# Two heads of dilated attention side by side, and one 512-column product for the values of two patterns

## The chip, the cores and the metric

The kernel runs on one core of a Trainium2 chip. The metric is the device time of one execution in microseconds (us), lower is better.

## The reference, cut to what matters

Two transformer-like layers of a first block run first, then a second block with an FFN, a mixing part and another FFN, all on 512 tokens of 1024 features in float32. The change lies in the mixing part of the second block, in its dilated attention:

```
ATTN_PATTERNS = ((128, 1), (512, 4), (2048, 16))     # window, dilation; 4 heads of 64 in each pattern
...
logits = jnp.einsum('bqghd,bgqkhd->bghqk', qb, kb) * scale + bias[None, :, :, None, :]
logits = jnp.where(valid[None, :, None], logits, -jnp.inf)
lse = jax.nn.logsumexp(logits, axis=-1)
probs = jnp.exp(logits - lse[..., None])
out = jnp.einsum('bghqk,bgqkhd->bqghd', probs, vb)
mix = jax.nn.softmax(lse, axis=1)
return jnp.einsum('bghq,bqghd->bqhd', mix, out).astype(q.dtype)
```

The queries, keys and values of the three patterns are columns of one projection `u @ w_in`: 256 columns (4 heads of 64) for each of the three, in each pattern.

## The kernel before, in words

Activations are kept transposed, features on the 128 partitions and 512 tokens along the row, as two parts `hi` and `lo` whose sum is the float32 value (tiles `hn` in the mixing part). Weights come from DRAM in pieces of 512 KB (`raw`), which ScalarE and VectorE split into `whi` and `wlo` (lines 259 and 260). A product of two split operands is three matmuls, lines 291, 292 and 293 (`three`).

`featmajor` gives a product with features on the partitions: a piece of the weights is what is loaded into the array (the stationary operand) and 512 tokens stream through. `tokmajor` gives a product with tokens on the partitions, which the values need: 128 tokens of `hn` are loaded into the array and 256 columns of the weights stream. For 8 slices of the features, 4 blocks of tokens and 3 matmuls that is 96 matmuls per pattern. The first pattern takes its blocks of 128 tokens as they stand. The second and third take every fourth token, so the loaded operand is read with a step of four elements:

```
view = None if p == 0 else (lambda a, tb: a.rearrange("p (i r) -> p r i", r=4)[:, tb, :])
```

`dilated(p)` works through a pattern's 4 heads, two to a tile `m`: the first head of the tile lies on partitions 0 to 63 and the second on 64 to 127. For each head and each block `b` of 128 queries there is one step: a float32 matmul for the logits (line 1425, contraction over 64 rows, 128 or 256 keys wide, called QK below), bias and row minimum on VectorE (line 1428), exponential on ScalarE (line 1430), a transposition on TensorE (line 489, one per 128 keys), a copy of it by ScalarE (line 1435), and the product with the values (line 1437, 64 columns of the array, called AV below). Each float32 matmul of QK and AV is two records in the trace. In all there are 48 QK (36 of 128 keys and 12 of 256) and 60 AV, in 36 groups of one and 12 groups of two.

Results in PSUM use eight banks: four in turn (`pj`) for the large products, two in turn (`lt`) for the logits and transpositions, one each for the others.

`together` sets the order in which the work is written down: the large products (`mix_products`) are its main line, and after each of them as many steps of the attention (one per 2.2 units of cost) and of the state space part (one per 5) are written as its cost pays for; a large product counts 10. A scheduler then fixes one order of instructions per engine. `shares` weighs the patterns' results at the end and hands them to the product `wup`, which is on the main line. Tiles of the tag `h` (eight in turn) hold a pattern's bias, Q, K and V.

Of the kernel before, what the change touches and what calls it, by code (L numbers as in the profile page):

```python
# [11 lines left out]
AF = mybir.ActivationFunctionType  # L12
# [5 lines left out]
P = 128  # L18
# [7 lines left out]
# ---------------------------------------------------------------- column orders  # L26
# [14 lines left out]
def first_chunks():  # L41
    """256 columns of w_in per chunk (-1 is a zero column), and each chunk's place."""
# [28 lines left out]
def chunked(w, n=256):  # L71
    """[K, M] -> [M / n, 128, K / 128 * n]: a chunk of n columns, contiguous per partition."""
    k, m = w.shape
    return np.ascontiguousarray(w.reshape(k // P, P, m // n, n).transpose(2, 1, 0, 3)).reshape(m // n, P, k // P * n)


def feat(v):
    """[K] or [..., K] -> [128, ..., K / 128]"""
    v = np.asarray(v)
    return np.ascontiguousarray(np.moveaxis(v.reshape(v.shape[:-1] + (v.shape[-1] // P, P)), -1, 0))  # L80


# columns of the constants and of the vectors
# [45 lines left out]
def onehots():  # L129
    """[33, 896]: which bucket lies at each place of the three patterns' bands (row 32: NEG where none does)"""  # L130
# [55 lines left out]
def prepare(x):  # L186
# [23 lines left out]
    out["win2"] = chunked(x["w_in"][0])  # L210
    out["fnrow"] = x["final_norm"].reshape(1, D)
# [11 lines left out]
# ---------------------------------------------------------------- the program  # L223
class Prog:
# [19 lines left out]
    # -- small helpers  # L244
# [4 lines left out]
    def weights(self, src, kt, n=256, held=False):  # L249
        """src: [128, kt * n] in DRAM -> the two exact parts, [128, kt, n] each."""  # L250
# [18 lines left out]
    # the eight banks: products, then small results in two rings, then sums that stay for long  # L269
# [18 lines left out]
    def three(self, ps, a, b, first, last, **kw):  # L288
        """ps += (a[0] + a[1])^T (b[0] + b[1]) without the lowest product."""
# [5 lines left out]
    def featmajor(self, src, hT, nk=8):  # L295
        """two tiles [128 columns, 512 tokens] of a chunk of 256 columns"""
# [9 lines left out]
    def tokmajor(self, src, hT, nk=8, view=None, grans=None):  # L306
        """two tiles [128 tokens, 2 blocks, 256 columns] of a chunk of 256 columns"""
# [10 lines left out]
    def rsqrt(self, v, n, pool):  # L318
        """v: [128, n] -> 1 / sqrt(v), by Newton's steps from the bits' halving"""
# [13 lines left out]
    def squares(self, acc, first, src, eng=None, **kw):  # L333
        """acc += src^2"""
# [8 lines left out]
    def sums(self, ps, acc, nb=NB):  # L343
        """acc's sums over the partitions, a column per block of 128 tokens"""
# [4 lines left out]
    def rms(self, acc, nb=NB):  # L349
        """1 / rms per token, as columns"""  # L350
# [5 lines left out]
    def spread(self, r, nb=NB, R=None):  # L356
        """a column per block -> the row on every partition"""
# [12 lines left out]
    def scaled(self, hi, lo, x, w):  # L370
        """the parts of x * w, w a column"""
# [3 lines left out]
    def h8(self, pool=None, tag="h"):  # L375
        """the parts of a transposed activation: [hi, lo][d]"""
# [11 lines left out]
    def setup(self):  # L388
# [19 lines left out]
        # the weights of the first block's last norm and of the one that follows it  # L408
# [3 lines left out]
    def normed(self, h, chunk, R, w):  # L412
        """h <- the parts of chunk * w * R"""
# [6 lines left out]
    # ------------------------------------------------------------ first block  # L420
    def layer(self, l, xs, x, z, acc, grans=None):
        """xs: x^T in DRAM, [128, 8, 512], x the same on chip, z the parts of x times the norm's weight, acc the sums
        of x's squares; the new x^T goes to xd"""
# [48 lines left out]
    def rope(self, x, nh, b0, nb=2):  # L472
        """x: [128, nb blocks from b0, nh, 64] in place, first 16 of each 64"""
# [17 lines left out]
    def scaled_copy(self, ps, j):  # L491
        """two blocks of a product of z, each token by its 1 / rms"""
# [6 lines left out]
    def stacked_q(self, src, scale, ps=None):  # L499
        """a chunk of 4 heads of 64 -> [128 = (hi, lo), 4, 512] of q^T, after rope"""  # L500
# [30 lines left out]
    def dsa_index(self, l, ps, pi):  # L531
# [7 lines left out]
        for j in range(2):  # L539
# [12 lines left out]
            for b in range(2):  # L552
# [4 lines left out]
                # the latent, normed  # L557
# [19 lines left out]
        # scores  # L577
# [20 lines left out]
    def dsa_choose(self):  # L598
        """the scores become 0 at the 128 chosen keys and NEG at the others"""
# [15 lines left out]
    def transposed(self, tb, src, PT):  # L615
        """src: [128 t, (tb + 1) * 128 s] -> the parts PT[s, sb, t]"""
# [9 lines left out]
    def stacked_av(self, V, PT):  # L626
        """V(sb): [128 s, 128 = (v_hi | v_lo)]; -> [128, 512]"""
# [7 lines left out]
    def values(self, V, ps, j):  # L635
        """ps: [128 t, 2 blocks, 4 heads * 64] -> V[:, 2 j + b, h, (hi | lo)]"""
# [5 lines left out]
    def heads_out(self, g, i, o, Y):  # L642
        """rows 0-63 + rows 64-127 of o -> Y[(i % 2) * 64..]"""
# [6 lines left out]
    def dsa(self, l, W, g):  # L650
# [17 lines left out]
        for h in range(4):  # L668
# [9 lines left out]
            for tb in range(NB):  # L678
# [7 lines left out]
                # the negated logits, and the least of them  # L686
# [68 lines left out]
    def ml_gates(self, l):  # L755
        """log decay sums, running maxima: for all four heads"""
# [7 lines left out]
        # log_sigmoid(f) = min(f, 0) - log1p(exp(-|f|))  # L764
# [20 lines left out]
        # sums from each block's start  # L785
# [9 lines left out]
        # g[s] in the frame of each later block  # L795
# [6 lines left out]
        # running maximum, as rows  # L802
# [20 lines left out]
    def mlstm(self, l, W, u):  # L823
# [32 lines left out]
        for e in range(2):  # L856
# [37 lines left out]
            # the variance of the quotients, and its root times the quotients' factor  # L894
# [9 lines left out]
    def ml_finish(self, l):  # L904
        """the last head's quotients, normed, to DRAM"""
# [14 lines left out]
    def branch(self, l, W, g, place):  # L920
        """the branch's gated output through its weights, times the merge gate, into mixed"""
# [49 lines left out]
    def layer_out(self, l, xs, mh):  # L971
# [19 lines left out]
        # two norms in a row  # L991
# [15 lines left out]
    # ------------------------------------------------------------ second block  # L1007
# [40 lines left out]
    def last(self, g):  # L1048
        """the last products, tokens on the partitions, and the last norm"""
# [12 lines left out]
        for c in range(4):  # L1062
            # the last chunk's weights stay, so that the last block of tokens can come after the others
# [25 lines left out]
    def last_rows(self, x, fn, ss, ps, c, tbs):  # L1089
        """the products ps of the blocks tbs, chunk c, to the residual; after the last chunk the norm and the result"""  # L1090
# [32 lines left out]
    def gated(self, c, th2, br, place, mh=None):  # L1123
        """adds 2 * sigmoid(pg) * br to the chunk's two tiles of mixed"""
# [258 lines left out]
    def dilated_qkv(self, W, p):  # L1383
# [21 lines left out]
        for j in range(2):  # L1405
            nc.scalar.copy(V[:, 2 * j:2 * j + 2, :], ps[j].rearrange("p (b c) -> p b c", b=2))
# [443 lines left out]
```

## Time and profile before

| | |
|---|---|
| three timed runs | 2649.14, 2650.55 (median), 2650.63 us |
| profiled execution, first to last instruction (its span) | 2647.3 us |
| median of the timed runs less that span | 3.25 us |
| TensorE busy | 2602.0 us, 98% of the span |
| VectorE busy | 1673.3 us, 63% |
| ScalarE busy | 1181.7 us, 45% |
| GpSimd busy | 267.4 us, 10% |
| chain of work that ended last | TensorE 76%, VectorE 8%, ScalarE 3% |
| DMA | 115 GB/s over the span |

The profile's busy time of TensorE is modelled: matmuls are pipelined, and a record lasts until its result is out, so that the records of neighbours overlap. How many matmuls the engine gets through is read from the distance between the starts of neighbours, not from the mean length of a record.

### The profile page before, as it was taken

The numbers are of one execution on the slowest core, as the hardware profiler recorded it, in microseconds if no ns is written. First come the engines' busy times: TensorE is split into PE (matmuls) and PEld (weight loads), VectorE is DVE, ScalarE is ACT, GpSimd is POOL, SyncE is SP. The second block draws the span as 40 slices with busy tenths as digits, with TensorE's granted clock in tenths as the row PEclk, the third lists the DMA queues.
The fourth block names the chain that finished last, engine by engine and source line by source line (L and its number), as shares of the span: only waits on it lengthen the run. The fifth ranks groups of instructions, "written<-read, shape, count | busy, mean of one in ns | idle before, by whom it ended". The sixth has DMA issues, their size and how long they took to land.

```text
span 2647.3 us, 36272 instructions
## 1 busy us (share of the span) xinstructions
PE 2602.0 (98%) x13302; PEld 2137.8 (81%) x13302; DVE 1673.3 (63%) x3696; ACT 1181.7 (45%) x2310; POOL 267.4 (10%) x573
## 2 busy tenths in 40 slices
PE   8999999999999999999999999999999999999998
PEld 8888778788888778878888888877876787888898
DVE  8999976644699997664588664373323444555523
ACT  6565656733566665763433332243333233333322
POOL 1010000110000000010004870000000100000000
PEclk9999999999999999999999999999999999999999
DMA  6232232353322223235333334353323454322332
GB/s 191 82 108 84 85 111 98 110 176 130 110 71 87 84 89 115 97 113 173 112 128 116 131 132 134 120 179 113 106 65 115 139 170 135 119 97 96 121 92 83
DMA packets 115106, 305.58 MB, mean 115 GB/s; under 512 B 29210, under 2 KB 36506, under 8 KB 114928
## 3 DMA queue, kind: packets, MB, share of 16 engines
q1 hardware_dynamic: 87760, 236.23, 27.6%
q0 software_dynamic: 18576, 60.17, 6.5%
q10 hardware_dynamic: 8592, 6.87, 0.8%
q8 instruction: 105, 1.72, 0.3%
q14 instruction: 73, 0.60, 0.1%
HBM read 259.41 MB, written 43.79 MB: 115 GB/s over the span
## 4 chain that ended last, share of the span: by engine, by line
PE 76%; DVE 8%; ACT 3%; issue 1%; DMA 1%; SPq 0%; ACTq 0%; DVEq 0%; POOLq 0%
PE b L291 22%; PE b L292 22%; PE b L293 22%; PE b L489 2%; DVE wlo L260 1%; PE b L632 1%; DVE row L744 1%; PE b L683 1%; PE b L1425 1%; PE b L1437 1%; DVE row L743 1%; DVE row L746 1%; DVE row L742 1%; DMA row<-xd 0%; DVE keep L606 0%
## 5 line engine op out<-in xcount | busy, mean ns | idle before, releaser
L260 DVE TENSOR_TENSOR wlo<-raw,whi 128x1024 fp32r<-128x1024 f32 (+1 forms) x398 | 481.1, 1209 | 500.1 <-ACT whi L259 498.6
L259 ACT CAST whi<-raw 128x1024 fp32r<-128x1024 f32 (+1 forms) x398 | 412.9, 1037 | 634.3 <-PE b L292 482.8
L291 PE MATMUL b<-h,whi 128*128 128x512 f32 x1632 | 642.1, 393 | 0.0
L292 PE MATMUL b<-h,whi 128*128 128x512 f32 x1632 | 641.7, 393 | 0.0
L293 PE MATMUL b<-h,wlo 128*128 128x512 f32 x1632 | 640.3, 392 | 0.4 <-DVE wlo L260 0.4
L291 PEld LDWEIGHTS b<-h,whi 128*128 128x128 f32 x1632 | 307.3, 188 | 61.8 <-issue 2.3
L293 PEld LDWEIGHTS b<-h,wlo 128*128 128x128 f32 x1632 | 307.1, 188 | 61.6 <-DVE wlo L260 0.8
L292 PEld LDWEIGHTS b<-h,whi 128*128 128x128 f32 x1632 | 307.1, 188 | 60.0 <-issue 1.3
L291 PE MATMUL b<-hn,whi 128*128 128x512 f32 x320 | 129.8, 405 | 0.3 <-ACT hn L246 0.3
L293 PE MATMUL b<-hn,wlo 128*128 128x512 f32 x320 | 129.4, 405 | 0.0
L292 PE MATMUL b<-hn,whi 128*128 128x512 f32 x320 | 128.5, 402 | 0.0
L292 PE MATMUL b<-wlo,h 128*128 128x256 f32 x384 | 109.5, 285 | 0.0
L293 PE MATMUL b<-whi,h 128*128 128x256 f32 x384 | 109.2, 284 | 0.0
L291 PE MATMUL b<-whi,h 128*128 128x256 f32 x384 | 109.1, 284 | 0.0
L489 PE MATMUL b<-cst,row 128*128 128x128 f32 x452 | 88.5, 285 | 15.4 <-DVE row L746 11.1
L489 PEld LDWEIGHTS b<-cst,row 128*128 128x128 f32 x452 | 52.1, 141 | 58.7 <-issue 16.9
L1024 ACT ACTIVATE row<-row 128x512 f32<-128x512 f32 x44 | 27.8, 632 | 122.9 <-DVE row L1023 99.1
L293 PE MATMUL b<-whi,g 128*128 128x256 f32 x288 | 81.9, 284 | 0.0
L291 PE MATMUL b<-whi,g 128*128 128x256 f32 x288 | 81.6, 284 | 0.0
L292 PE MATMUL b<-wlo,g 128*128 128x256 f32 x288 | 81.6, 283 | 0.0
L291 PE MATMUL b<-yb,whi 128*128 128x512 f32 x192 | 75.9, 396 | 0.0
L293 PE MATMUL b<-yb,wlo 128*128 128x512 f32 x192 | 75.6, 394 | 0.0
(590 smaller groups left out, 5337.4 us busy)
## 6 DMA issues: line engine op xcount, KB each, us to landing
raw<-in_win_dram SPq DMA_DIRECT2D x194, 512.0 KB, 3.8
raw<-in_ffn_in_dram SPq DMA_DIRECT2D x88, 512.0 KB, 3.7
raw<-in_ffn_down_dram SPq DMA_DIRECT2D x40, 512.0 KB, 3.5
raw<-in_wbr_dram SPq DMA_DIRECT2D x24, 512.0 KB, 3.5
mxd<-fr POOLq DMA_DIRECT2D x48, 256.0 KB, 2.4
fr<-mxd POOLq DMA_DIRECT2D x48, 256.0 KB, 3.7
raw<-in_wout_dram SPq DMA_DIRECT2D x24, 512.0 KB, 3.7
yd<-row POOLq DMA_DIRECT2D x24, 256.0 KB, 2.6
```

The source lines that it names most:

```text
L259: nc.scalar.copy(hi, raw)
L260: nc.vector.tensor_sub(lo, raw, hi.bitcast(F32))
L291: mm(ps, a[0], b[0], start=first, stop=False)
L292: mm(ps, a[0], b[1], start=False, stop=False)
L293: mm(ps, a[1], b[0], start=False, stop=last)
L489: self.nc.tensor.transpose(out, in_, self.c("ident"))
L632: self.nc.tensor.matmul(o[:, c], V(sb), PT[i][:, sb, c], start=sb == 0 and i == 0, stop=sb == 3 and i == 1)
L683: nc.tensor.matmul(p[:, :nn], Q[h][:, tb * P:(tb + 1) * P], kk[i][:, :nn], start=i == 0, stop=i == 1)
L742: nc.vector.scalar_tensor_tensor(e[:, :n], e[:, :n], 1.0, st[:, :n], op0=ALU.min, op1=ALU.mult)
L743: nc.vector.scalar_tensor_tensor(sg[:, :n], sg[:, :n], 0.0, e[:, :n], op0=ALU.max, op1=ALU.add)
L744: nc.vector.tensor_tensor_scan(e[:, :n][:, ::-1], st[:, :n][:, ::-1], self.one.to_broadcast([P, n]), 1.0, op0=ALU.mult, op1=ALU.min)
L1024: nc.scalar.activation(th, t, AF.Tanh, scale=0.5)
```

## The change

The host lays the value weights of the second and third pattern out once more, as one matrix of 512 columns (`wv12`). A new function `values12` makes both patterns' values in one product at the place of the second pattern's: each loaded block of 128 tokens now meets 512 streaming columns instead of 256, over four banks of `pj` at once, and the third pattern has no value product of its own. `dilated` handles the two heads of a tile in one step, split over two turns of `together`: in the first both QK into two `lt` banks, the minimum and the exponential of each; in the second the transpositions of both into one bank, one copy for both, and the AV of both, alternating between the array's column halves 0 to 63 and 64 to 127. Comments were also taken out, which shifts line numbers by one to thirty; lines of the new kernel are 292 to 294 for the three matmuls, 1447 for QK, 490 for the transposition and 1466 for AV.

```diff
+    out["wv12"] = chunked(x["w_in"][0][:, 256 * 9:256 * 11], 512)[0]
...
-        view = None if p == 0 else (lambda a, tb: a.rearrange("p (i r) -> p r i", r=4)[:, tb, :])
-        ps = self.tokmajor(W[8 + p], self.hT, view=view)
-        V = self.m4(shape=(NB, 256))
-        for j in range(2):
-            nc.scalar.copy(V[:, 2 * j:2 * j + 2, :], ps[j].rearrange("p (b c) -> p b c", b=2))
-        self.dil[p] = (*qk, V, bias)
+        if p == 0:
+            ps = self.tokmajor(W[8], self.hT)
+            V = self.m4(shape=(NB, 256))
+            for j in range(2):
+                nc.scalar.copy(V[:, 2 * j:2 * j + 2, :], ps[j].rearrange("p (b c) -> p b c", b=2))
+            self.dv = [V]
+            yield 10.0
+        elif p == 1:
+            yield from self.values12()
+        self.dil[p] = (*qk, self.dv[p], bias)
         self.have.add(f"d{p}")
+
+    def values12(self):
+        nc = self.nc
+        V = [self.m4(shape=(NB, 256)) for _ in range(2)]
+        ps = [self.pj() for _ in range(NB)]
+        at = [h.rearrange("p (i r) -> p r i", r=4) for x in self.hT for h in x]
+        for i, gran in enumerate(self.granules(self.A["wv12"], 8, n=512, g=2)):
+            for tb in range(NB):
+                for k, hi, lo in gran:
+                    self.three(ps[tb], (at[k][:, tb, :], at[8 + k][:, tb, :]), (hi, lo), k == 0, k == 7)
+            if i % 2 == 1 and i < 3:
+                yield 10.0
+        for tb in range(NB):
+            for e in range(2):
+                nc.scalar.copy(V[e][:, tb, :], ps[tb][:, 256 * e:256 * e + 256])
+        self.dv += V
         yield 10.0
...
-            for e2 in range(2):
-                h = 2 * m + e2
-                r = slice(64 * e2, 64 * e2 + 64)
-                for b in range(NB):
-                    k0, n = (b * P, P) if p or b == 0 else ((b - 1) * P, 256)
-                    ps = self.lt()
-                    nc.tensor.matmul(ps[:, :n], Q[r, m, b * P:(b + 1) * P], K[r, m, k0:k0 + n], start=True, stop=True)
...
+            for b in range(NB):
+                k0, n = (b * P, P) if p or b == 0 else ((b - 1) * P, 256)
+                ps = [self.lt() for _ in range(2)]
+                for e in range(2):
+                    r = slice(64 * e, 64 * e + 64)
+                    nc.tensor.matmul(ps[e][:, :n], Q[r, m, b * P:(b + 1) * P], K[r, m, k0:k0 + n], start=True, stop=True)
+                L = self.row()
+                for e in range(2):
+                    h = 2 * m + e
+                    Le = L[:, e * n:(e + 1) * n]
...
-                    for j in range(n // P):
-                        nc.tensor.matmul(o[r, b * P:(b + 1) * P], V[:, k0 // P + j, h * 64:(h + 1) * 64], T[:, j * P:(j + 1) * P],
-                                         start=j == 0, stop=j == n // P - 1)
-                    yield True
...
+                yield True
+                ps = self.lt()
+                for j in range(2 * n // P):
+                    self.tr(ps[:, j * P:(j + 1) * P], L[:, j * P:(j + 1) * P])
+                T = self.row()
+                nc.scalar.copy(T[:, :2 * n], ps[:, :2 * n])
+                nj = n // P
+                for j in range(nj):
+                    for e in range(2):
+                        h = 2 * m + e
+                        nc.tensor.matmul(o[64 * e:64 * e + 64, b * P:(b + 1) * P], V[:, k0 // P + j, h * 64:(h + 1) * 64],
+                                         T[:, (e * nj + j) * P:(e * nj + j + 1) * P], start=j == 0, stop=j == nj - 1)
+                yield True
```

How this stands in the order of instructions is shown at two places. The first is TensorE's order at the start of the second pattern's value product, in the kernel before (the streaming operand is named first, the loaded one second, then the size of the result):

```order
L291 MATMUL b_3355_18387<-whi_18391,hn_17105 128x256
L292 MATMUL b_3355_18387<-wlo_18392,hn_17105 128x256
L293 MATMUL b_3355_18387<-whi_18391,hn_17109 128x256
L291 MATMUL b_3355_18387<-whi_18391,hn_17105 128x256
L292 MATMUL b_3355_18387<-wlo_18392,hn_17105 128x256
```

The same engine at the start of the shared value product, in the changed kernel:

```order
L292 MATMUL b_3313_18281<-whi_18287,hn_17105 128x512
L293 MATMUL b_3313_18281<-wlo_18288,hn_17105 128x512
L294 MATMUL b_3313_18281<-whi_18287,hn_17109 128x512
L292 MATMUL b_3313_18281<-whi_18287,hn_17105 128x512
L293 MATMUL b_3313_18281<-wlo_18288,hn_17105 128x512
```

Of such rows there were 192 in the second and third pattern's products, and there are 96 now, twice as wide.

The second place is TensorE's order in the third pattern's attention, in the kernel before (`b` is a PSUM bank, `cst` the identity of a transposition, `row` an exponential or its transposed copy, `h` the tiles of Q, K and V):

```order
L1425 MATMUL b_3585_19455<-h_18799,h_18660 128x128
L293 MATMUL b_3593_19475<-hn_17106,wlo_19480 128x512
L489 MATMUL b_3578_19414<-cst_58,row_19411 128x128
L291 MATMUL b_3594_19476<-hn_17105,whi_19479 128x512
L292 MATMUL b_3594_19476<-hn_17109,whi_19479 128x512
L1437 MATMUL b_3563_19378<-row_19416,h_19005 64x128
L1425 MATMUL b_3589_19465<-h_18799,h_18660 128x128
L293 MATMUL b_3594_19476<-hn_17105,wlo_19480 128x512
L489 MATMUL b_3587_19460<-cst_58,row_19457 128x128
L291 MATMUL b_3594_19476<-hn_17105,whi_19479 128x512
L292 MATMUL b_3594_19476<-hn_17109,whi_19479 128x512
L1437 MATMUL b_3563_19378<-row_19462,h_19005 64x128
```

And TensorE's order in the third pattern's attention in the changed kernel:

```order
L1447 MATMUL b_3492_19171<-h_18814,h_18651 128x128
L293 MATMUL b_3500_19196<-xk_19014,whi_19200 128x512
L490 MATMUL b_3490_19164<-cst_58,row_19093 128x128
L294 MATMUL b_3500_19196<-xk_19012,wlo_19201 128x512
L292 MATMUL b_3501_19197<-xk_19011,whi_19200 128x512
L293 MATMUL b_3501_19197<-xk_19013,whi_19200 128x512
L1466 MATMUL b_3471_19072<-row_19167,h_18280 64x128 x2
L1447 MATMUL b_3493_19172<-h_18814,h_18651 128x128
L490 MATMUL b_3495_19180<-cst_58,row_19175 128x128
```

Two AV that stood apart now stand together (x2). The two QK of a pair (banks 3492 and 3493) do not: the second stands behind the AV of the pair before, since it takes the bank in which that pair's transpositions were (there are two in the `lt` ring). Over all of TensorE's order the two QK of a pair are neighbours in 4 of 24 pairs, the AV stand in 18 groups of two and 6 of four, and a QK stands directly behind an AV at 18 places, where it was 23. Ahead of the attention of the first pattern and behind the start of `shares` the order of TensorE's instructions is the same in both kernels.

## Rows read from the trace of the kernel before

**Rows 1.** The page's first line: span and instructions

```profile
span 2647.3 us, 36272 instructions
```

**Rows 2.** Windows, the mixing part: length, then each engine's busy us, clock, DMA

```profile
1800.00:2060.00 260.00, 257.93 (x1185) 190.71 (x1184) 89.89 (x244) 94.24 (x245) 3.24 (x6) 0.99 0.32 98
```

**Rows 3.** Groups by line, TensorE, same stretch: one of three equal groups

```profile
L292 PE MATMUL b<-wlo,hn 128*128 128x256 f32 x64 | 26.1, 409 | 0.0
```

**Rows 4.** Timeline, TensorE, first pattern's values: first and last of 81 records

```profile
1789.91 0.28 PE L291 MATMUL b<-whi,hn 128*128 128x256 f32 x1
...
1799.52 0.28 PE L293 MATMUL b<-whi,hn 128*128 128x256 f32 x1
```

**Rows 5.** Timeline, TensorE, third pattern's values: first and last of 40 records

```profile
1931.99 0.40 PE L292 MATMUL b<-wlo,hn 128*128 128x256 f32 x1
...
1941.10 0.40 PE L292 MATMUL b<-wlo,hn 128*128 128x256 f32 x1
```

**Rows 6.** Groups by line, weight loads: 1788 to 1799 us, first pattern's values

```profile
L291 PEld LDWEIGHTS b<-whi,hn 128*128 128x128 f32 x30 | 5.6, 188 | 0.0
```

**Rows 7.** Groups by line, weight loads: 1868 to 1874 us, second pattern's values

```profile
L291 PEld LDWEIGHTS b<-whi,hn 128*128 128x128 f32 x7 | 2.3, 326 | 0.0
```

**Rows 8.** Timeline, TensorE, 512 columns: first and last of 10 records

```profile
2036.07 0.39 PE L292 MATMUL b<-hn,whi 128*128 128x512 f32 x1
...
2038.15 0.39 PE L292 MATMUL b<-hn,whi 128*128 128x512 f32 x1
```

**Rows 9.** Timeline, TensorE: a QK alone between large products

```profile
2039.69 0.40 PE L293 MATMUL b<-xk,wlo 128*128 128x512 f32 x1
2040.01 0.49 PE L1425 MATMUL b<-h,h 64*128 64x128 f32 x2
2040.43 0.50 PE L291 MATMUL b<-xk,whi 128*128 128x512 f32 x1
2040.77 0.39 PE L292 MATMUL b<-xk,whi 128*128 128x512 f32 x1
```

**Rows 10.** Timeline, TensorE: one AV (two records) alone

```profile
2041.57 0.39 PE L292 MATMUL b<-xk,whi 128*128 128x512 f32 x1
2041.89 0.43 PE L1437 MATMUL b<-row,h 128*64 128x128 f32 x2
2042.25 0.50 PE L293 MATMUL b<-xk,wlo 128*128 128x512 f32 x1
2042.59 0.39 PE L291 MATMUL b<-xk,whi 128*128 128x512 f32 x1
```

**Rows 11.** Timeline, TensorE: two AV of the same head (four records)

```profile
1830.78 0.65 PE L1437 MATMUL b<-row,h 128*64 128x128 f32 x4
```

**Rows 12.** Timeline, TensorE: a QK directly behind an AV

```profile
1917.64 0.43 PE L1437 MATMUL b<-row,h 128*64 128x128 f32 x2
1918.00 0.48 PE L1425 MATMUL b<-h,h 64*128 64x128 f32 x2
1918.42 0.51 PE L293 MATMUL b<-hn,wlo 128*128 128x512 f32 x1
```

**Rows 13.** Timeline: a QK and the exponential of its result

```profile
2015.19 0.48 PE L1425 MATMUL b<-h,h 64*128 64x128 f32 x2
...
2016.41 0.40 ACT L1430 ACTIVATE row<-row,st 128x128 f32<-128x128 f32 x1
```

**Rows 14.** Timeline: waits around 2002 us, waiting time and releaser in brackets

```profile
2002.28 1.04 ACT L259 CAST whi<-raw 128x1024 fp32r<-128x1024 f32 x1 [4.52 <-PE b L292]
...
2003.55 0.43 PE L1437 MATMUL b<-row,h 128*64 128x128 f32 x2 [1.07 <-ACT row L1435]
...
2004.85 0.48 PE L1425 MATMUL b<-h,h 64*128 64x128 f32 x2 [0.87 <-DVE st L1428]
```

**Rows 15.** Windows, behind those waits (columns as in rows 2)

```profile
2006.00:2009.00 3.00, 2.98 (x9) 1.57 (x7) 0.77 (x3) 1.72 (x6) 0.00 (x0) 0.50 0.41 156
```

More of the change, by code (lines that the diff above doesn't have):

```diff
@@ L1418, in dilated @@
             o = self.av()
-            for e2 in range(2):
-                h = 2 * m + e2
-                r = slice(64 * e2, 64 * e2 + 64)
-                for b in range(NB):
-                    k0, n = (b * P, P) if p or b == 0 else ((b - 1) * P, 256)
-                    ps = self.lt()
-                    nc.tensor.matmul(ps[:, :n], Q[r, m, b * P:(b + 1) * P], K[r, m, k0:k0 + n], start=True, stop=True)
-                    L = self.row()
+            for b in range(NB):
[8 more added lines that the diff above has]
+                    Le = L[:, e * n:(e + 1) * n]
@@ L1427, in dilated @@
                     st = st2[:, b, 0, h:h + 1]
-                    nc.vector.tensor_tensor_reduce(L[:, :n], ps[:, :n], bias[:, h, nb - n:], op0=ALU.add, op1=ALU.min,
+                    nc.vector.tensor_tensor_reduce(Le, ps[e][:, :n], bias[:, h, nb - n:], op0=ALU.add, op1=ALU.min,
                                                    accum_out=st, scale=-1.0, scalar=3.0e38)
-                    nc.scalar.activation(L[:, :n], L[:, :n], AF.Exp, bias=st, scale=-1.0, accum_out=st2[:, b, 1, h:h + 1])
@@ L1431, in dilated @@
-                    ps = self.lt()
-                    for j in range(n // P):
-                        self.tr(ps[:, j * P:(j + 1) * P], L[:, j * P:(j + 1) * P])
-                    T = self.row()
-                    nc.scalar.copy(T[:, :n], ps[:, :n])
-                    for j in range(n // P):
-                        nc.tensor.matmul(o[r, b * P:(b + 1) * P], V[:, k0 // P + j, h * 64:(h + 1) * 64], T[:, j * P:(j + 1) * P],
-                                         start=j == 0, stop=j == n // P - 1)
@@ L1439, in dilated @@
-                    yield True
+                    nc.scalar.activation(Le, Le, AF.Exp, bias=st, scale=-1.0, accum_out=st2[:, b, 1, h:h + 1])
+                yield True
[10 more added lines that the diff above has]
+                                         T[:, (e * nj + j) * P:(e * nj + j + 1) * P], start=j == 0, stop=j == nj - 1)
```

## The prediction

> **What bounds the kernel now.** I read the page first: a span of 2647.3 us [rows 1], with TensorE busy nearly all of it. The change touches one stage only, so I then read the windows of that stage, 1800 to 2060 us: TensorE is busy for 257.93 of 260 us at full clock (0.99), VectorE and ScalarE for about 90 us each [rows 2]. TensorE sets the end here. What it no longer has to do comes off the time, as long as its order holds no new waits. VectorE and ScalarE have room.
>
> Busy time alone would mislead about sizes, because records of pipelined matmuls overlap. So I went to the timeline and took distances between starts.
>
> **The value products.** The first pattern's values, whose tokens are loaded as they stand, start every (1799.52 - 1789.91) / 80 = 0.120 us [rows 4]. The third pattern's matmuls are the same size (256 streaming columns), but their loaded operand is read with a step of four elements. They start every (1941.10 - 1931.99) / 39 = 0.234 us [rows 5]. Only the load differs, and it is longer: 326 ns as against 188 ns [rows 6, 7]. So these 192 matmuls (3 x 64, [rows 3]) are held up by their loads; streaming 256 columns would let them start every 0.120 us.
>
> Matmuls with 512 columns and ordinary loads start every (2038.15 - 2036.07) / 9 = 0.231 us [rows 8]. Streaming 512 columns therefore takes as long as a stepped load, and loads run beside the streaming of the matmul before. The new product needs 96 stepped loads under 96 streams of 512 columns.
>
> - Before: 192 x 0.234 = 44.9 us.
> - After, load under stream: 96 x 0.234 = 22.5 us. Saved: 22.4 us.
> - Lower bound of the gain: the extra of a stepped load (0.234 - 0.120 = 0.114) adds to the 0.231 in full. Then 96 x 0.345 = 33.1 us, saved 11.8 us.
> - Upper bound: the stream alone counts, 96 x 0.231 = 22.2 us, saved 22.7 us.
>
> I take 22.4, because rows 5 show the load as the longer of two things that overlap, not as an addition.
>
> The Trainium skill has a rule that speaks against this gain. "TensorE: Matmul & The Clock Gate", section "LDWEIGHTS (loading the stationary operand)", gives a load's time by its columns alone, P / 1.2 ns, about 107 ns for 128, whatever the layout. By it an estimate of the saving would be 192 x 0.120 - 96 x 0.231 = 0.9 us. The trace does not agree: 326 ns against 188 ns at equal columns. The page "SBUF — State Buffer", section "Door 1: The DMA port swizzle", says that each access that crosses to a new 16-byte line pays; a step of four float32 is 16 bytes, and the trace agrees with that.
>
> The rest of this part costs nothing that shows. The same four pieces of 512 KB are read and split. One piece still serves 24 matmuls of 0.23 us, as in every other large product, so the weights need not come faster. Evictions become eight copies of 256 columns for four of 512. The next product's first bank is free once the first block of tokens is copied out, and that block ends 18 matmuls, 4.2 us, before the product does. The second V tile takes the place of the first pattern's bias, whose last reader stands well ahead in the order. Without that cover the next product would wait for two copies, under 1 us.
>
> **The attention steps.** Costs of insertions, from the start of the last large matmul before to the start of the second one after, less two ordinary distances of 0.231 us:
>
> - One AV alone: 2042.59 - 2041.57 - 0.46 = 0.56 us [rows 10].
> - Two AV of one head together: their records last 0.65 us instead of 0.43 us [rows 10, 11], so 0.56 + 0.22 = 0.78 us. A further AV in the group costs 0.22 us.
> - A QK of 128 keys alone: 2040.77 - 2039.69 - 0.46 = 0.62 us [rows 9].
> - A QK directly behind an AV: it starts 0.36 us after the AV and the large product 0.42 us after the QK [rows 12], the same distances as in rows 9 and 10. What falls away is one way out of the small shape and one way in: the large matmul after starts 0.34 us before the next instead of 0.23 [rows 9], and the one before likewise, together 0.2 us.
>
> Before, AV cost 36 x 0.56 + 12 x 0.78 = 29.5 us. After, there are 18 groups of two and 6 of four.
>
> - If the second half waits for the first as in rows 11: 18 x 0.78 + 6 x (0.78 + 2 x 0.22) = 21.4 us, saved 8.1 us.
> - If the halves run fully beside each other, a group of two costs what one costs: 18 x 0.56 + 6 x 0.78 = 14.8 us, saved 14.7 us.
>
> No row shows two halves of the array in use together. I take the middle, 11.4 us. The Trainium skill, "TensorEngine Tiling (Array Packing)", section "Key Properties", states that tiles operate independently and load and multiply in parallel. By that the 14.7 would hold; no run here shows it.
>
> The QK keep their number and mostly their cost, since only 4 of 24 pairs are neighbours: 4 x 0.2 = 0.8 us saved at least, 4 x 0.62 = 2.5 us at most. Places where a QK follows an AV fall from 23 to 18, which costs 5 x 0.2 = 1.0 us. Transpositions keep their number. ScalarE has 24 copies fewer, which is cover that nobody waits for.
>
> **New waits.** A pair's second QK now stands close ahead of the transposition that needs its exponential. In the rows of the order shown, a transposition and three or four large matmuls lie between, about 1.1 us. In the trace the way from the end of a QK (2015.67) to the end of its exponential (2016.81) is 1.14 us with the engines free [rows 13]. Ten of the 24 pairs stand so, and I price each at 0 to 0.4 us; I take 2 us in all, with 0 and 4 as bounds. TensorE's large products queue behind such a wait.
>
> The one long wait of this stage stays where it is: a cast of weights on ScalarE waits for TensorE to release a buffer, the copy of a transposition stands behind it, and TensorE waits 1.07 and 0.87 us [rows 14], after which the clock stands at half for 3 us [rows 15]. That is about 2 + 1.5 us. The changed order has two such casts ahead of an exponential at the same product, so I cost it at nothing, with 3.5 us either way as bounds.
>
> **The sum.** 22.4 + 11.4 + 0.8 - 1.0 - 2.0 = 31.6 us off the profiled execution's span of 2647.3 us. The median of the timed runs lies 3.25 us above that span, and I let that stand: 2650.55 - 31.6 = 2619 us.
>
> **The rivals.**
>
> 1. *The stepped load is not hidden under 512 columns.* Then the first part gives 11.8 and the time is about 2630 us. For it: nowhere in the trace does a stepped load meet 512 columns. Against it: rows 5 and 6, where ordinary loads vanish under 0.120 us. Chance 0.12.
> 2. *The slow spacing belongs to the product, not to the load.* Then 512 columns take 0.468 us each, the first part saves nothing, and the time is about 2641 us. The skill's rule of a load by columns alone would lead here. Against it: rows 7. Chance 0.04.
> 3. *The PSUM ring makes TensorE wait.* A pair needs both `lt` banks for its QK and one again for its transpositions, so the second QK waits for the pair before. To end slower than before by 0.2%, about what a measurement of this kernel can tell from no change (5.3 us), 37 us must be lost: 1.5 us for each of 24 pairs. A single wait of 1.07 us is the longest that the stage shows now [rows 14], and the ring has three turns per pair where it had four. At 2 us a pair the time would be 2619 + 46 = 2665 us (48 in place of the 2 allowed). Chance 0.03.
> 4. *The same waits, smaller.* At 0.6 us a pair, 14 us in place of 2, the time is 2631 us. Chance 0.08.
>
> If the halves of the array don't run side by side at all, only 3.3 us of the forecast go (2622 us); that is part of the forecast.
>
> **How the numbers follow.** The forecast, both gains with small waits, has 0.73. Its own range takes the bounds: most gain 22.7 + 14.7 + 2.5 - 1.0 + 3.5 = 42.4 (2608 us), least with hidden loads 22.4 + 8.1 + 0.8 - 1.0 - 4 - 3.5 = 22.8 (2628 us). The range given, 2608 to 2632, takes in rivals 1 and 4 as well; rivals 2 and 3 and the tails of 1 and 4 stay outside, under 2 in 10. Faster by over 0.2%: 0.95 (all but rival 3 and a small tail of 2 and 4); within: 0.02; slower: 0.03.
>
> **What would show each step.** In the changed kernel's timeline the shared value product starts every 0.23 to 0.24 us (0.345 for rival 1, 0.47 for rival 2). A group of two AV lies between 0.43 and 0.65 us long as a merged row. Waits of TensorE for ScalarE's exponential (now line 1455) before line 490 sum to about 2 us. The stage from the first QK to the last of `shares` is some 30 us shorter, and stages before and behind keep their length. The prediction is wrong if TensorE's clock falls in new places, or if waits before lines 490 or 1447 reach tens of us.

## The result, and the profile after

The changed kernel takes 2615.88 us (median of four runs, 2614.03 to 2617.0) where the kernel before took 2650.26 us beside it. The ratio is 0.9867, with a 95% interval from 0.9854 to 0.988. The forecast was 2619 us with a range of 2608 to 2632; of the 34.4 us that came off, 31.6 were forecast.

The page's first line, span and instructions (before: [rows 1]):

```profile
span 2613.5 us, 36025 instructions
```

Windows, the mixing part of the changed kernel and a short stretch inside it (columns as in [rows 2]):

```profile
1800.00:2030.00 230.00, 228.43 (x1125) 170.12 (x1124) 88.54 (x242) 93.89 (x227) 3.78 (x7) 1.00 0.37 112
2041.00:2043.50 2.50, 2.50 (x6) 1.96 (x7) 2.50 (x4) 0.47 (x1) 0.00 (x0) 0.50 0.34 105
```

TensorE is as full as before (228.43 of 230 us), VectorE and ScalarE have as much room. So the time came off as work that TensorE no longer has, and nothing else took its place as the bound. The second row is a stretch at half clock, which will matter below.

Timeline of the changed kernel, TensorE. First a QK in front of the shared value product and the product itself (line numbers are one higher than before: the value matmuls are lines 292 to 294, QK is line 1447, AV line 1466), then a group of four AV, a group of two, and two QK that are neighbours:

```profile
1856.81 0.70 PE L1447 MATMUL b<-h,h 64*128 64x256 f32 x2
1857.43 0.63 PE L292 MATMUL b<-whi,hn 128*128 128x512 f32 x1
1857.90 0.40 PE L293 MATMUL b<-wlo,hn 128*128 128x512 f32 x1
1858.13 0.40 PE L294 MATMUL b<-whi,hn 128*128 128x512 f32 x1
...
1862.42 0.39 PE L294 MATMUL b<-whi,hn 128*128 128x512 f32 x1
...
1867.51 0.66 PE L1466 MATMUL b<-row,h 128*64 128x128 f32 x8
...
1945.98 0.40 PE L293 MATMUL b<-hn,whi 128*128 128x512 f32 x1
1946.31 0.44 PE L1466 MATMUL b<-row,h 128*64 128x128 f32 x4
1946.68 0.50 PE L294 MATMUL b<-hn,wlo 128*128 128x512 f32 x1
1947.02 0.39 PE L292 MATMUL b<-hn,whi 128*128 128x512 f32 x1
...
1951.32 0.49 PE L1447 MATMUL b<-h,h 64*128 64x128 f32 x4
```

- **Value product.** From 1858.13 to 1862.42 there are 19 records one behind the other, so they start every 4.29 / 18 = 0.238 us with twice the columns. Before it was 0.234 for half of them [rows 5].
- **AV on two halves.** The group of two (x4 records) costs 1947.02 - 1945.98 - 0.46 = 0.58 us. One AV alone cost 0.56 [rows 10]. The group of four lasts 0.66 as a merged row, about what two AV of one head lasted before (0.65, [rows 11]).
- **QK on two halves.** The pair (x4) lasts 0.49, as a single one does [rows 9].

The waits of TensorE from 1800 to 2070 us (waiting instruction, releaser, us in total, times, longest):

```profile
PE b L490 <- ACT row L1455: 1.3, 1, 1.3
PE b L1501 <- DVE row L1509: 0.9, 1, 0.9
PE b L292 <- ACT xk L1254: 0.2, 1, 0.2
```

The waits of [rows 14] are gone. In their place a transposition waits once for an exponential, the matmuls of `shares` (line 1501) wait once for VectorE, and a large matmul waits briefly for ScalarE.

### The profile page after: what moved, and what is told of

Same layout as the page of the kernel before. It is cut to its first block, busy times and chain, and to the rows that moved or that the text cites. A ratio compares the mean times of both kernels' runs of the same rounds, so it can differ in the third digit from the quotient of the medians.

```text
span 2613.5 us, 36025 instructions
## 1 busy us (share of the span) xinstructions
PE 2568.2 (98%) x13206; PEld 2113.5 (81%) x13206; DVE 1673.0 (64%) x3696; ACT 1179.3 (45%) x2290; POOL 265.9 (10%) x573
## 4 chain that ended last, share of the span: by engine, by line
PE 75%; DVE 8%; ACT 3%; issue 1%; DMA 1%; SPq 0%; ACTq 0%; DVEq 0%; POOLq 0%
PE b L292 22%; PE b L293 22%; PE b L294 22%; PE b L490 3%; DVE wlo L261 1%; PE b L633 1%; DVE row L745 1%; PE b L684 1%; PE b L1447 1%; DVE row L744 1%; DVE row L747 1%; DVE row L743 1%; DMA row<-xd 0%; DVE keep L607 0%; PE b L1466 0%
```

## The experiments

### All runs in one table

Two executions of one kernel differ by some us in their profiles, and most of the reason is visible: stretches in which TensorE is granted half its clock, 3.41 us or more each. The column "half clock" sums the stretches ahead of 2600 us whose granted clock reads 0.50 in the windows. At the very end, behind 2600 us, every profile has one more such stretch, of 2.5 to 5.6 us, in which no matmul runs; that part is left in. The last column is the span less half of the column before it, an estimate of the same execution at full clock. It supposes that TensorE sets the pace in those stretches; in the changed kernel the large matmuls from 2041.41 to 2043.54 us do stand 0.43 us apart, and 0.23 elsewhere.

| kernel | median us | ratio to before on its chip | profiled span | half clock | span at full clock |
|---|---|---|---|---|---|
| before | 2650.26 | | 2647.3 | 6.8 | 2643.9 |
| before_again | 2653.70 (one run) | | 2651.8 | 13.7 | 2645.0 |
| changed kernel | 2615.88 | 0.9867 [0.9854, 0.988] | 2613.5 | 10.2 | 2608.4 |
| after_again | 2615.22 | 0.9867 [0.9854, 0.9881] | 2611.9 | 6.8 | 2608.5 |
| values_only | 2631.66 | 0.9916 [0.9902, 0.993] | 2630.4 | 10.2 | 2625.3 |
| values_again | 2632.83 | 0.9931 [0.9918, 0.9944] | 2632.5 | 13.7 | 2625.7 |
| heads_only | 2633.06 | 0.9922 [0.9909, 0.9934] | 2631.4 | 6.8 | 2628.0 |
| heads_again | 2634.75 | 0.994 [0.9927, 0.9954] | 2638.2 | 20.5 | 2628.0 |
| before_plain_loads | 2628.37 | 0.9901 [0.9886, 0.9917] | 2633.1 | 20.5 | 2622.8 |
| same_half | 2621.63 | 0.9883 [0.9869, 0.9897] | 2623.8 | 20.5 | 2613.5 |
| own_fetch | 2614.47 | 0.9859 [0.9845, 0.9872] | 2615.3 | 13.7 | 2608.5 |
| values_fetch | 2632.00 | 0.9924 [0.9912, 0.9937] | 2629.4 | 13.7 | 2622.5 |
| qk_py_bank | 2614.70 | 0.9861 [0.9846, 0.9876] | 2609.8 | 10.2 | 2604.6 |
| plain_loads_after | 2615.60 | 0.9861 [0.9847, 0.9874] | 2615.5 | 17.1 | 2606.9 |

The spans at full clock of two profiles of one kernel agree within 1.1 us for before and within 0.4 us for the other three, though their spans differ by up to 6.8 us. That makes the last column a finer measure than one span, but not an exact one. TensorE's order up to the first value matmul of the first pattern is the same in all fourteen profiles. The timeline, TensorE, at that matmul, before first and values_again second:

```profile
1786.89 0.36 PE L291 MATMUL b<-whi,hn 128*128 128x256 f32 x1
1788.61 0.36 PE L292 MATMUL b<-whi,hn 128*128 128x256 f32 x1
```

No stretch at half clock that the column counts lies ahead of it in either, and still they are 1.7 us apart. So a difference of 1 to 4 us in the last column can lie in part outside of what an edit changed.

### Each part alone: values_only and heads_only

values_only has `values12` of the changed kernel and the attention loop of the kernel before:

```diff
         for m in range(2):
             o = self.av()
-            for b in range(NB):
...
-                ps = [self.lt() for _ in range(2)]
+            for e2 in range(2):
+                h = 2 * m + e2
+                r = slice(64 * e2, 64 * e2 + 64)
+                for b in range(NB):
...
+                    ps = self.lt()
```

> Only the shared value product of the change; the attention steps are those of the kernel before. If a stepped load hides under 512 streaming columns (the profile after shows starts 0.238 us apart), 192 x 0.234 - 96 x 0.238 = 22.1 us come off: about 2628 us. If the value product owes part of its gain to the new attention steps (fewer insertions in it, fewer waits), clearly less: under 18 us, above 2632 us.

heads_only has the attention loop of the changed kernel and, for the second and third pattern, the 256-column products of the kernel before:

```diff
-        elif p == 1:
-            yield from self.values12()
...
+        view = None if p == 0 else (lambda a, tb: a.rearrange("p (i r) -> p r i", r=4)[:, tb, :])
```

> Only the attention steps of the change; each pattern has its own value product as before. If the two halves of the array run beside each other, a group of two AV costs what one cost: 14.7 us, and 2.5 us for neighbouring QK, less 1.0 us for fewer QK behind an AV and some 2 us of waits: 12 to 16 us off, 2634 to 2638 us. If the halves take turns and only the ways in and out of the small shape are saved, 6 to 9 us off: 2641 to 2644 us.

By their ratios they took 22.3 and 20.7 us off. Neither gain is absent, so rival 2 of the prediction falls. Together, though, they took more than the whole (35), while the profiled spans gave only 16.9 and 15.9 against the span of before. So one thing was open: do the parts add up? The timeline of values_only, TensorE, at the matmuls of `shares` (line 1494 there) showed a place at which its own gain was partly given back:

```profile
2057.53 2.38 PE L1494 MATMUL b<-row,cst 4*128 4x512 f32 x4 [1.16 <-DVE row L1502]
...
2060.44 0.63 PE L292 MATMUL b<-hn,whi 128*128 128x512 f32 x1
2060.86 0.63 PE L293 MATMUL b<-hn,whi 128*128 128x512 f32 x1
```

A wait of 1.16 us, and behind it large matmuls that start 0.42 us apart in place of 0.23: half clock, for 6.8 us here.

### What a stepped load costs: before_plain_loads

```diff
-        view = None if p == 0 else (lambda a, tb: a.rearrange("p (i r) -> p r i", r=4)[:, tb, :])
+        view = None
```

> The kernel before, with the second and third pattern's value products loading blocks of 128 neighbouring tokens instead of every fourth one, so that these values belong to other tokens. If the step of the load sets the spacing of 0.234 us, it falls to 0.120 us, loads to 188 ns, and 192 x 0.114 = 21.9 us come off: about 2628 us, as much as the 512-column product gives. If the spacing belongs to the product, nothing changes: 2650 us.

Timeline of this kernel, TensorE, second pattern's values: the first and last of 39 records one behind the other.

```profile
1921.35 0.28 PE L293 MATMUL b<-whi,hn 128*128 128x256 f32 x1
...
1925.86 0.28 PE L292 MATMUL b<-wlo,hn 128*128 128x256 f32 x1
```

They start every 4.51 / 38 = 0.119 us in place of 0.234 [rows 5], and at full clock the kernel is 21.7 us shorter than before (mean of that kernel's two profiles, 2644.5). The step of the load alone doubled the time of these products. The shared product gains the same amount by another way: it does not make the load shorter, it puts twice the columns over it.

### Whether the halves run together: same_half

The changed kernel, with the AV of both heads in the same column half of the array, one head behind the other; the other half of the output is zero:

```diff
+            nc.vector.memset(o[64:128, :], 0.0)
-                for j in range(nj):
-                    for e in range(2):
+                for e in range(2):
+                    for j in range(nj):
...
-                        nc.tensor.matmul(o[64 * e:64 * e + 64, b * P:(b + 1) * P], V[:, k0 // P + j, h * 64:(h + 1) * 64],
+                        nc.tensor.matmul(o[0:64, b * P:(b + 1) * P], V[:, k0 // P + j, h * 64:(h + 1) * 64],
```

> The changed kernel with the AV of both heads written to column half 0 to 63 of the array, one head after the other (the second head's rows replace the first's, the other half is set to zero). If the overlap of the halves makes the gain, a group of two takes 0.65 us as a merged record and costs 0.78 us instead of 0.57: 18 x 0.21 + 6 x 0.43 = 6.4 us more than the changed kernel, about 2622 us. If only the grouping makes it, no change: 2616 us.

Timeline, TensorE, a group of two AV:

```profile
1948.07 0.40 PE L292 MATMUL b<-hn,whi 128*128 128x512 f32 x1
1948.40 0.65 PE L1467 MATMUL b<-row,h 128*64 128x128 f32 x4
1948.98 0.50 PE L293 MATMUL b<-hn,whi 128*128 128x512 f32 x1
1949.32 0.39 PE L294 MATMUL b<-hn,wlo 128*128 128x512 f32 x1
```

The same four records cost 1949.32 - 1948.07 - 0.46 = 0.79 us on one half and 0.58 on two. At full clock the kernel is 5.1 us longer than the changed one; by the ratios it is 4.2 us longer, but the intervals overlap (0.9869 to 0.988), so the timeline is the firmer evidence. A group of two costs what one AV costs only when its AV stand on two halves: there they run beside each other.

"TensorEngine Tiling (Array Packing)", section "Key Properties", of the Trainium skill says that tiles work independently and in parallel; the trace agrees with it here (0.58 against 0.56 us for one).

### The wait in `shares`: own_fetch and values_fetch

Both take the tiles into which `shares` fetches the stored results from the `h` ring, and fetch them at its start:

```diff
+        od = []
+        for p in range(3):
+            od.append(self.m4())
+            nc.sync.dma_start(od[p], self.od[:, 2 * p:2 * p + 2, :])
...
-                o = self.fr()
-                nc.sync.dma_start(o, self.od[:, 2 * p + m, :])
+                o = od[p][:, m, :]
```

own_fetch is the changed kernel with this edit:

> The changed kernel, with the tiles into which `shares` fetches the stored results of the three patterns taken from the free places of the `h` ring, all three fetched at its start, in place of six tiles of the ring that the gates use too. Theory: in the changed kernel VectorE waited 3.13 us for such a fetch, TensorE 0.9 us for VectorE behind it, and 3.4 us at half clock stand behind that wait; with the fetches early the wait goes, and with it the half clock: 0.9 + 1.7 = 2.6 us less than the changed kernel. Rival: the half clock follows the small matmuls of `shares` (4 rows of the array) and not the wait; then 0.9 us less at most, and the clock falls near the same place. Second rival: the new bounds of the ring make other work wait, same time or slower.

Timeline of own_fetch, TensorE's rows of `shares` (lines 490 and 1505):

```profile
2024.47 1.98 PE L1505 MATMUL b<-row,cst 4*128 4x512 f32 x4
...
2027.84 1.98 PE L1505 MATMUL b<-row,cst 4*128 4x512 f32 x4
...
2030.10 0.77 PE L490 MATMUL b<-cst,sh 128*4 128x128 f32 x4 [0.29 <-DVE row L1512]
...
2032.51 3.78 PE L1505 MATMUL b<-row,cst 4*128 4x512 f32 x4
```

And its windows:

```profile
2031.00:2033.50 2.50, 2.50 (x5) 1.16 (x5) 1.89 (x3) 0.55 (x1) 0.54 (x1) 0.50 0.02 7
```

The wait went (0.29 is left of 0.89), and the time did not. In this profile the clock fell at 2030.4 us all the same, for 10.2 us, where a stretch of 3.4 us stood behind the wait in the changed kernel. The last four records of small matmuls took 3.78 us in place of 1.98. So the first rival held as far as one profile shows it: in this stage the half clock does not need the wait. What stands before it here are eight records of matmuls that use 4 rows of the array, close together. That the edit caused the longer stretch is not shown: same_half and plain_loads_after, in which `shares` keeps its wait, have a stretch of 10.2 us there too (from 2034.9 and 2024.3 us on).

values_fetch is values_only with the same edit:

> Only the shared value product, with the attention of the kernel before (as values_only), and the early fetches of own_fetch. values_only took 15.3 us off the stage in its profile where the value product alone should give 22; it showed a wait of 1.2 us in `shares` and two stretches of 3.4 us or more at half clock there. Theory: what was missing stands at that place, so with the fetches early the stage's gain rises by 1.2 + 1.7 to 1.2 + 3.4 us, 3 to 4.6 us less than values_only. Rival: what was missing lies in the value product itself or in the insertions around it; then 1 us less at most.

At full clock it is 3.0 us shorter than values_only (2622.5 against 2625.5, the mean of two). Not all of that is the edit's: at full clock the first value matmul of the first pattern, far ahead of `shares`, starts 1.4 us earlier than in those two (at 1788.86 us, less 1.7 for a stretch at half clock ahead of it, against 1788.55 and 1788.61). What is left, 1.6 us, is little more than the wait of 1.16 us. Its stretch at half clock behind `shares` lasts 10.2 us, and the timed runs show no gain (0.9924 against 0.9916 and 0.9931). The theory fell here too: that the half clock goes with the wait was wrong.

### More neighbours among the QK: qk_py_bank

```diff
-                ps = [self.lt() for _ in range(2)]
+                ps = [self.lt(), self.bank("py")]
```

> The changed kernel, with the second head's QK of a pair in the bank `py`, so that it need not wait until the pair before has left the `lt` ring. The two QK of a pair are then neighbours in 10 of 24 pairs (4 before), but a QK stands directly behind an AV at 7 places (18 before). Theory (neighbours on two halves cost as much as one, 0.62 us): 6 x 0.62 = 3.7 us saved, 11 x 0.2 = 2.2 us given back, so 1.5 us less than the changed kernel. Rival: halves save only the way in and out (0.2 us a pair), then 1 us more. Both are near what can be told apart; what the adjacent QK cost is read in the timeline.

Timeline, TensorE, a pair of QK between large matmuls:

```profile
1952.48 0.40 PE L294 MATMUL b<-hn,wlo 128*128 128x512 f32 x1
1952.81 0.49 PE L1447 MATMUL b<-h,h 64*128 64x128 f32 x4
1953.23 0.50 PE L292 MATMUL b<-hn,whi 128*128 128x512 f32 x1
1953.56 0.39 PE L293 MATMUL b<-hn,whi 128*128 128x512 f32 x1
```

Two QK on two row halves cost 1953.56 - 1952.48 - 0.46 = 0.62 us, what one cost [rows 9]. So the row halves run beside each other here, as the column halves do. The kernel is 3.8 us shorter than the changed one at full clock, of which not all need be the edit's, and its timed median (2614.70) is no different from those of own_fetch and plain_loads_after on the same chip (2614.47, 2615.60). Whether it is faster stays open. No version here beats the changed kernel by more than the measurement can tell.

### What is left of the stepped load: plain_loads_after

```diff
-        at = [h.rearrange("p (i r) -> p r i", r=4) for x in self.hT for h in x]
+        at = [h for x in self.hT for h in x]
...
-                    self.three(ps[tb], (at[k][:, tb, :], at[8 + k][:, tb, :]), (hi, lo), k == 0, k == 7)
+                    self.three(ps[tb], (at[k][:, tb * P:(tb + 1) * P], at[8 + k][:, tb * P:(tb + 1) * P]), (hi, lo), k == 0, k == 7)
```

> The changed kernel, with the value product's tokens loaded as they stand and not with a step of four elements, so that the values of the second and third pattern belong to other tokens (what is computed is changed, the number and shape of the instructions is not). Theory: the stepped load is hidden under 512 columns, so matmuls start every 0.231 to 0.235 us where they started every 0.238, 0.7 us less at most in 96, and up to 2 us where a load stands behind an insertion and has no stream over it. Rival: the load still adds in full at many places, then 5 us less or more.

Timeline, TensorE, the same place as in the changed kernel: a QK, the product behind it, and the last of 19 records that follow each other from 1858.73 us.

```profile
1857.54 0.70 PE L1447 MATMUL b<-h,h 64*128 64x256 f32 x2
1858.16 0.50 PE L292 MATMUL b<-whi,hn 128*128 128x512 f32 x1
1858.50 0.39 PE L293 MATMUL b<-wlo,hn 128*128 128x512 f32 x1
1858.73 0.39 PE L294 MATMUL b<-whi,hn 128*128 128x512 f32 x1
...
1862.92 0.39 PE L294 MATMUL b<-whi,hn 128*128 128x512 f32 x1
```

In a run of matmuls the spacing is 4.19 / 18 = 0.233 us, so the stepped load costs 0.238 - 0.233 = 0.005 us there: it is hidden. Behind an insertion it is not quite: the second value matmul starts 0.34 us after the first (1858.50 - 1858.16) with plain loads, and 0.47 (1857.90 - 1857.43) with stepped ones. The same shows at ten more places of the product: from the first matmul behind an insertion to the second it takes 0.11 or 0.12 us more than with plain loads. For the eleven places together that is 1.3 us. In all the kernel is 1.5 us shorter at full clock, and the timed runs (0.9861 against 0.9867) can't tell the two apart.

### The parts and the whole on one chip: after_again, values_again, heads_again, before_again

These are the changed kernel, the two parts and the kernel before, unchanged.

> The changed kernel once more, on one chip with its two parts alone. On the first chip the parts took 22.3 and 20.7 us off by their ratios, 43 together, and the whole took 35 off on another. By the spacings the parts give 22 (value product) and 14.7 + 2.5 - 1.0 = 16 (attention), 38 together, less 2 to 3 us of waits and half clock. Theory: the parts add up, and the first chip's runs of the kernel before lay 3 to 4 us high; then whole = sum of the parts within 3 us here. Rival: the parts take something from each other (the same idle time ended by both), then the whole stays 6 us or more short of the sum here too.

> Only the shared value product, once more (as values_only), on one chip with the whole. Theory: 19 to 20 us less than the kernel before (22 less one wait more and a stretch more at half clock). Rival: 22 us or more, and then the whole has lost something of it.

> Only the two heads side by side, once more (as heads_only), on one chip with the whole. Theory: 15 to 17 us less than the kernel before. Rival: 20 us or more, and then the whole has lost something of it.

> The kernel before once more, for a second profile of it. Theory: what ends up at half clock is the same place in each execution (behind the long waits near 2005 us); then the stretches stand where they stood, at 2005, 2227 and 2644 us. Rival: the places differ between executions of the same kernel, and with them the length of a stage by 1.7 us for each; then differences of 2 to 4 us between single profiles tell nothing.

On one chip, against 2650.7 us, the value product took 17.9 us off, the heads 16.0, and the whole 35.5. The sum of the parts is 33.9, 1.6 short of the whole. At full clock the parts give 19.0 and 16.5, together 35.5, and the whole 36.0. The timed runs can be put at full clock too, if each span is multiplied by its granted clock: the means are 2642.5 us for the kernel before (26 runs on three chips), 2622.8 for the value product alone (9), 2626.1 for the heads alone (10) and 2606.3 for the whole (8). They lie some 2 us below the column of the table, since here the end counts as at full clock too. So the parts give 19.7 and 16.4, together 36.1, and the whole 36.2. The parts add up. The surplus on the first chip came for the most part from its runs of the kernel before: their median was 2654.26 us, 3.6 above the 2650.7 here, and it counts in both parts.

The second half of the question, why single spans differ, shows in two profiles of the same kernel. The cores of heads_only and of heads_again, span and mean granted clock:

```profile
core 0: 2631.4 us, clock 0.998
```

```profile
core 0: 2638.2 us, clock 0.995
```

And one window at which they differ, heads_only first:

```profile
1951.00:1953.00 2.00, 2.00 (x12) 1.58 (x12) 0.28 (x2) 0.53 (x3) 0.00 (x0) 1.00 0.00 0
```

```profile
1951.00:1953.00 2.00, 2.00 (x11) 2.00 (x9) 0.00 (x0) 0.76 (x3) 0.00 (x0) 0.50 0.00 0
```

heads_again has six stretches of 3.41 us where heads_only has two. Half of the four more is 6.8 us, the whole difference of the spans. The kernel before has two in one profile (at 2005.6 and 2227.5 us) and four in the other (at 150.5, 2007.3, 2065.4 and 2232.6). So the rival held in part: the places near 2006 and 2230 us came back, others came and went.

## Why the prediction was right

**What bounds the kernel.** Right. TensorE was full before and after, and what left it came off the time.

**The value products, 22.4 us.** Right, with a small remainder. By the spacing of 0.238 us, 96 matmuls take 22.9 us, so 22.0 come off; the load lies under the stream, and rival 1 (0.345 us) and rival 2 (0.468) fall. The 1.3 us of stepped loads behind insertions (plain_loads_after) were not foreseen. Alone, in values_only, the product gives 19.0 at full clock by the profiles and 19.7 by the timed runs; the new wait in `shares` there, 1.2 to 1.4 us in the two profiles, accounts for most of what is missing from 20.7. One reading of the prediction is loose: for ordinary loads that vanish under 0.120 us it names rows 5 and 6, but the spacing of 0.120 is that of rows 4, and a load's record in rows 6 lasts 0.188 us, longer than that spacing.

**AV on two halves, 11.4 us.** The mechanism, two halves side by side, was right and the size was off. The step that missed reads "No row shows two halves of the array in use together. I take the middle". By these rows the halves overlap almost fully: 18 x 0.58 + 6 x 0.80 = 15.2 us (the group of four as 0.58 + 0.66 - 0.44), so 29.5 - 15.2 = 14.3 came off, next to the upper bound of 14.7. same_half, which puts them on one half, gives 5.1 us back at full clock; the prediction's two bounds lie 14.7 - 8.1 = 6.6 apart.

**Neighbouring QK, 0.8 us.** Mis-sized in the same way. Two cost what one costs (qk_py_bank), so the 4 pairs save 4 x 0.62 = 2.5 us, the upper bound.

**Fewer QK behind an AV, 1.0 us lost.** No run tested it by itself.

**New waits, 2 us lost.** Mis-sized. The waits of the changed kernel sum to 1.3 + 0.9 + 0.2 = 2.4 us, but 1.5 of them are the long wait of [rows 14] (1.07 + 0.87 = 1.94) in another form: of the ten places at which the second exponential stands close, one waited, at the same cast that ScalarE has ahead of it. At the other nine TensorE did not wait. New is the 0.9 us in `shares`, which the prediction did not name. Net 0.5 us. Rivals 3 and 4 fall.

**The half clock, costed at nothing.** Right in the sum: 10.2 and 6.8 us of it in the two profiles of the changed kernel, 6.8 and 13.7 in those of the kernel before. That it came out even is luck. The prediction looked at one stretch, behind the long wait, and expected it to stay. It is in both profiles of the kernel before and in neither of the changed kernel, while own_fetch, with the same 1.29 us of wait, has it (from 1972.4 us on). In turn both profiles of the changed kernel have a stretch near 2041 us, behind the wait in `shares`. By the prediction's own sign, "if TensorE's clock falls in new places", it would have been wrong. The sign was badly chosen, since places differ between two profiles of one kernel as well.

**The sum.** 22.0 - 1.3 + 14.3 + 2.5 - 1.0 - 0.5 = 36.0 us, and at full clock the profiles give 36.0, the timed runs 36.2; as single profiles scatter by more than a us and the 1.0 is not tested, so close a match is luck in part. The prediction's 31.6 was short by what the halves of the array gave, 2.9 us at AV and 1.7 at QK; what it missed in the value products (22.4 - 20.7 = 1.7) and in the waits (2.0 - 0.5 = 1.5) nearly cancels, which is luck. That stages ahead and behind keep their length was right too, to 1 or 2 us and except for stretches at half clock that come and go.

## What to carry to other kernels

A load of the stationary operand that is longer than the stream over it can be hidden by widening the stream, as here from 256 to 512 columns: look for products whose starts are farther apart than their columns explain, and join products that load the same thing. Small matmuls that use half of the array cost hardly more in pairs on both halves than alone (0.58 against 0.56 us for AV, 0.62 against 0.62 for QK), if the order puts them side by side; count the neighbours in the order, not the pairs in the code. Before comparing single profiles to a few us, add up in each the stretches at half clock: here that took two profiles of one kernel from 6.8 us apart to under 0.1. A us or two can be left even so.

## What the runs showed of the hardware

- Stretches at half clock come at different places, and in different numbers, in two executions of the same kernel (two and six ahead of 2600 us for the heads alone), and each of 3.41 us costs an estimated 1.7 us. TensorE was busy without a gap in the two windows of heads_only and heads_again shown above.
- The same wait stands before a stretch at half clock in one execution and not in another: behind waits of 1.06 and 0.87 us near 1981 us the clock fell in values_again (0.50 from 1982 to 1985 us) and not in values_only, which is the same kernel (1.00 in the same window).
- Taking away a wait did not take away the half clock behind it. In `shares`, with its small matmuls of 4 rows closer together and no wait over 0.3 us, the stretch was 10.2 us long where it was 3.4 in the changed kernel (own_fetch, one profile each). Why was not settled: plain_loads_after, whose `shares` still has a wait, has a stretch of 10.2 us too, at 2024.3 us.
- A stepped load behind an insertion delays the second matmul of the run and not the first: 0.47 us between the two in place of 0.34, while from the QK to the first it is 0.62 us either way.
